# Gates and branch projections with tokens on partitions, in a two-layer hybrid encoder on one core

## The chip, the cores and the metric

The kernel runs on one core of a Trainium2 chip. The metric is the device time of one execution in microseconds (us). The engines named here are TensorE (PE, matmuls; PEld is its weight load), VectorE (DVE), ScalarE (ACT), GpSimd (POOL) and SyncE (SP, which here issues nearly all DMA transfers). Each engine works through its own list of instructions in order and waits on semaphores where it needs another engine's result.

## The reference

Two layers over 256 tokens of width 1024, in float32. Each layer has a token mixer and a gated MLP, each with an RMSNorm ahead and a residual sum behind. The mixer, which is the part that matters here:

```python
u, q, k, v, g_pool, g_attn = jnp.split(xn @ w_in, SPLITS, axis=-1)
pool_out = einsum(centred means of u at windows 2, 4, 8, 16, minus u; w_pool) * pool_scale
# three groups of four heads, (window, dilation) = (128,1), (512,4), (2048,16)
logits = q . k over +-64 strided keys / sqrt(128) + T5 bias;  p = softmax(logits)
attn = sum over the groups of softmax(lse over the groups) * (p @ v)      # 256 x 512
merged = sigmoid(g_pool) * (pool_out @ w_a) + sigmoid(g_attn) * (attn_out @ w_b)
h = h + merged @ w_o
```

The MLP is `(gelu(conv3(a)) * gval) @ w_down` with `a, gval` from `xn @ w_up`.

## The kernel before

**Arithmetic.** Every float32 operand of a large product is split in two parts, a rounded one (`h` in a name, for high) and the rest (`l`, low), and three products stand for one: high by high, high by low, low by high. The weights are split on the chip: a load of 1 MB lands in one of three `raw` buffers, ScalarE casts a piece of 128x1024 to `wh` (L177), VectorE subtracts to give `wl` (L178). Two pieces come from one load, and there are five `wh`/`wl` buffers; `W.get` hands out the next piece and splits up to three ahead, in the order in which `W.use` listed them.

**Layouts.** A product can leave its result in one of two layouts. In `proj` (L491 and L493, in `two_sums`) the weights are stationary and the tokens stream: the result has 128 channels on partitions and 256 tokens along the row, 8 matmuls with 512 columns and 8 with 256. In `v_sum` (L588) the normed tokens `x2` are stationary and the weights stream: the result has 128 tokens on partitions and 512 channels along the row. Tokens are split by parity: t = 0 holds the even ones, t = 1 the odd ones.

**Order of a layer.** Values (`v_sum`); the pool branch's `u`; then the queries and keys by `PAIRS`, two heads a visit; the four heads of attention; the projection of the pool branch by w_a into `pa`; the pool gate; the attention gate with the product by w_b; `residual_mm` with w_o; the norm; the MLP.

**Attention.** Four steps per head hh (each head stands for three, one of each group). `scores` (L886, L891) makes logits on TensorE, and VectorE and ScalarE make the softmax (L897, L902, L905, L908). `turn` transposes inside 32x32 blocks on VectorE (L915) into `rows` and then `cross` moves the blocks between groups of partitions by 16 transfers within SBUF, 32 KB each, all issued by SP (L598), into `pt`. `parts` casts and subtracts (L929, L930). `weigh` multiplies by the values (L939, L943) into `at2`. A list `steps` holds them as scores a, scores b, turn a, parts a, weigh a, turn b, parts b, weigh b for the pairs (0, 1) and (2, 3), and `step()` takes the next one after a projection. There is one `rows` and one `pt` buffer.

**Gates and merge.** `gate(c)` makes 128 channels of a gate by `proj`, adds the two sums (`add_up`: L513 on ScalarE, L514 on VectorE) and takes tanh (L1009); sigmoid is (tanh(x/2) + 1)/2, with the halves folded into the pool scale and the softmax scaling. The pool side is multiplied at L1014. For the attention side the product by w_b is made for 128 channels at a time (`b_ps`), multiplied (L1030), added to `pa` (L1033) and split into `mh`, `ml` (L1035, L1036). So the merged rows arrive with channels on partitions, as `residual_mm` (L518 to L520, `res_ps`) wants them: stationary operands of 128 channels by 128 tokens. `residual_mm` takes its eight channel blocks k in order: for k = 0 to 3 all four sums (two parities, two halves of the width); it holds k = 4 to 7 and finishes one sum after another, so that the norm can begin with the first (L423, then `xn` at L450 and the turn at L459).

**What orders the work.** The Python program says what follows what, and the framework's planner, which goes by its own costs, fixes each engine's list when the kernel is built; it may place instructions of one step between those of another. SP's list is in order too: a load that waits for its buffer holds back all transfers behind it. A transfer also waits for the transfer eight before it, which used the same semaphore.

Of the kernel before, what the change touches and what calls it, by code (L numbers as in the profile page):

```python
# [16 lines left out]
P = 128  # L17
D = 1024
# [20 lines left out]
LAG = 6  # L39
ENTRY = 4  # L40
# [164 lines left out]
def encoder(ctx, tc, x, w_in, w_pool, pool_scale, w_a, w_b, w_o, norm1, norm2, w_up, conv_w,  # L205
# [29 lines left out]
    for l in range(DEPTH):  # L235
# [10 lines left out]
        for n, c in enumerate(PAIRS):  # L246
            pool = ([], [])
            if n == 1:
                pool = W.add(
                    w_pool[l].rearrange("g (k p) c -> p (g k) c", p=P), (8, 256),  # L250
                    [((lambda t, j=j: t[:, 4 * j : 4 * j + 4, :]), (4, 256)) for j in range(2)],
                )
                pool = (pool[:1], pool[1:])
            W.use(pool[0] + cols(w_in[l], C_Q + c * 256))
            W.use(pool[1] + cols(w_in[l], C_K + c * 256))
        for c in range(4):
            W.use(cols(w_a[l], c * 256))
        for c in range(4):
            W.use(cols(w_in[l], C_GP + c * 256))
        for c in range(2):  # L260
            W.use(cols(w_in[l], C_GA + c * 512))
            W.use(cols(w_in[l], C_GA + c * 512 + 256))
            src = w_b[l][:, c * 512 : (c + 1) * 512].rearrange("(k p) c -> p k c", p=P)
            W.use(
                W.add(
                    src, (4, 512),
                    [((lambda t, j=j: t[:, :, j * 256 : (j + 1) * 256]), (4, 256)) for j in (0, 1)],
                )
            )
# [313 lines left out]
    def v_sum(ps, x2, t, n, piece):  # L583

        _, (wh, wl) = piece
        passes = [(0, wh, 0), (0, wl, 0), (1, wh, 0), (0, wh, 1), (0, wl, 1), (1, wh, 1)]
        for m, (part, w, j) in enumerate(passes):
            nc.tensor.matmul(  # L588
                ps, x2[:, 2 * n + j, part, t, :], w[:, j, :], start=(n + m == 0),
                stop=(n == 3 and m == 5),  # L590
            )

    def cross(out, in_):

        for i in range(4):
            for j in range(4):
                a, b = slice(32 * i, 32 * i + 32), slice(32 * j, 32 * j + 32)
                nc.sync.dma_start(out=out[b, i], in_=in_[a, j])  # L598

# [165 lines left out]
    for l in range(DEPTH):  # L765
# [113 lines left out]
        probs, ptiles = {}, {}  # L879
# [32 lines left out]
        def turn(hh):  # L912
# [6 lines left out]
            pt = sm.tile([P, 4, 2, 4, 32], F32, tag="pt", bufs=1, name="pt")  # L919
            cross(pt, rows)  # L920
            ptiles[hh] = pt
# [29 lines left out]
        steps = []  # L951
        for a, b in ((0, 1), (2, 3)):
            steps += [(scores, a), (scores, b), (turn, a), (parts, a), (weigh, a)]
            steps += [(turn, b), (parts, b), (weigh, b)]

        def step():
            if steps:
                f, *which = steps.pop(0)
                f(*which)


        for m, c in enumerate(PAIRS):
# [7 lines left out]
            for n in range(4):  # L970
                if m == 1:
                    next(pool_parts)
                src, rest = (halves(a) for a in proj(x2))
# [19 lines left out]
                if m >= 3 and n and len(steps) > 8:  # L993
                    step()

        pa = big.tile([P, KD, S], F32, tag="ybig", name="pa")
        for c in range(KD):
            add_up(pa[:, c, :], proj(po2))
            step()
        assert not steps  # L1000
# [3 lines left out]
        gates = big.tile([P, 4, S], F32, tag="gates", name="gates")  # L1004

        def gate(c):
            th = gates[:, c % 4, :]
            add_up(th, proj(x2))
            nc.scalar.activation(th, th, AF.Tanh, scale=0.5)  # L1009
            return th  # L1010

        for c in range(KD):
            th = gate(c)
            nc.vector.scalar_tensor_tensor(  # L1014
                out=pa[:, c, :], in0=th, scalar=1.0, in1=pa[:, c, :], op0=ALU.add, op1=ALU.mult
            )
        m2 = big.tile([P, 2, KD, 2, P], F32R, tag="m2", name="m2")
        mh, ml = m2[:, 0], m2[:, 1]
        for c4 in range(2):
            ths = [gate(4 * c4 + j) for j in range(4)]  # L1020
            for j2 in range(2):
                i, (wh, wl) = W.get()
                for j in range(2):
                    c = 4 * c4 + 2 * j2 + j
                    ps = mmp.tile([P, 2, S], F32, tag="mm", name="b_ps")
                    cc = slice(j * P, (j + 1) * P)
                    two_sums(ps, lambda k: wh[:, k, cc], lambda k: wl[:, k, cc], at2, 4)
                    m = sm.tile([P, S], F32, tag="u", name="m")
                    add_up(m, (ps[:, 0], ps[:, 1]))
                    nc.vector.scalar_tensor_tensor(  # L1030
                        out=m, in0=ths[2 * j2 + j], scalar=1.0, in1=m, op0=ALU.add, op1=ALU.mult
                    )
                    nc.vector.tensor_add(out=m, in0=m, in1=pa[:, c, :])  # L1033
                    m = halves(m)
                    nc.scalar.copy(out=mh[:, c], in_=m)  # L1035
                    nc.vector.tensor_sub(out=ml[:, c], in0=m, in1=mh[:, c].bitcast(F32))  # L1036
                W.free(i)
# [154 lines left out]
```

## Time and profile before

| | |
|---|---|
| median of 3 runs | 887.76 us (885.21 to 887.93) |
| the profiled execution | 886.05 us, span 884.3 us |
| TensorE busy | 868.0 us (98%) |
| VectorE, ScalarE busy | 682.5 us (77%), 518.7 us (59%) |
| DMA | 168.86 MB, mean 191 GB/s; queue q1's packets take 57% of 16 engines' span |

The page's groups have one line each: source line, engine, operation, output <- input, partitions x elements, count; then the busy time in us, the mean of one in ns, and the idle time of that engine just ahead of it with what ended it. A chain follows the work that ended last back to its causes: start, length, what. "SPq" is time in which SP issues transfers. By stretch, each engine has its busy time and, in brackets, its number of instructions; PEclk is the granted share of TensorE's clock. Matmuls overlap: one of 128x512 shows 0.39 us while the next starts 0.23 us behind it, so starts are to be compared, not lengths.

### The profile page before, as it was taken

What the parts mean: (1) busy time and instruction counts of PE and PEld (TensorE: products, weight loads), DVE (VectorE), ACT (ScalarE), POOL (GpSimd) and SP (SyncE); (2) the same over time, 40 slices, a digit from 0 to 9 for tenths busy, and PEclk for the clock granted to TensorE, in tenths of its full rate; (3) what the DMA queues carried; (4) which work ended last, traced back from release to release, by engine and by line L of the source; (5) the groups of instructions that cost most, each with busy time, mean ns of one, the idle gap of its engine ahead of it and who ended that gap; (6) DMA issues with size and microseconds to landing.
All of it is one profiled execution on the core that took longest, in us unless ns stands there. A gap on an engine that the chain in (4) does not pass through costs nothing.

```text
span 884.3 us, 12920 instructions
## 1 busy us (share of the span) xinstructions
PE 868.0 (98%) x4778; PEld 752.8 (85%) x4778; DVE 682.5 (77%) x1150; ACT 518.7 (59%) x905; POOL 14.7 (2%) x45
## 2 busy tenths in 40 slices
PE   9999999999999999999999999999999999999997
PEld 7888887888888888888888898888888888888886
DVE  6997785857869987787756977776678698878774
ACT  6755553556648766666545564554566486656653
POOL 2000000000000000000000000000000000000000
PEclk9999999999999999999999999999999999999999
DMA  9669636466564665565626465544755447556541
GB/s 326 214 232 297 226 117 196 157 222 208 179 207 146 208 219 191 165 215 191 238 96 237 144 215 168 170 164 135 269 188 191 158 155 247 182 191 199 182 143 49
DMA packets 132236, 168.86 MB, mean 191 GB/s; under 512 B 5302, under 2 KB 112518, under 8 KB 132044
## 3 DMA queue, kind: packets, MB, share of 16 engines
q1 hardware_dynamic: 132156, 168.02, 57.0%
q8 instruction: 38, 0.62, 0.3%
q14 instruction: 26, 0.21, 0.1%
q10 hardware_dynamic: 16, 0.00, 0.0%
HBM read 162.74 MB, written 3.69 MB: 188 GB/s over the span
## 4 chain that ended last, share of the span: by engine, by line
PE 82%; SPq 8%; DMA 3%; DVE 3%; issue 1%; ACT 1%; ACTq 0%; POOLq 0%; POOL 0%; DVEq 0%
PE proj_ps L491 30%; PE proj_ps L493 16%; SPq L598 8%; PE res_ps L518 6%; PE v_ps L588 6%; PE res_ps L519 6%; PE res_ps L520 6%; PE v_ps L757 2%; PE b_ps L491 2%; DMA pt<-rows 2%; PE v_ps L670 1%; DMA raw<-in_w_in_dram 1%; PE o_ps L939 1%; PE o_ps L943 1%; PE b_ps L493 1%
## 5 line engine op out<-in xcount | busy, mean ns | idle before, releaser
L178 DVE TENSOR_TENSOR wl<-raw,wh 128x1024 fp32r<-128x1024 f32 x274 | 333.8, 1223 | 121.5 <-ACT wh L177 119.6
L177 ACT CAST wh<-raw 128x1024 fp32r<-128x1024 f32 x274 | 286.1, 1049 | 183.0 <-PE proj_ps L491 113.6
L491 PE MATMUL proj_ps<-x,wh 128*128 128x512 f32 x1408 | 353.2, 392 | 0.0
L491 PEld LDWEIGHTS proj_ps<-x,wh 128*128 128x128 f32 x1408 | 254.1, 189 | 46.0
L493 PEld LDWEIGHTS proj_ps<-x,wl 128*128 128x128 f32 x1408 | 192.5, 190 | 13.8
L493 PE MATMUL proj_ps<-x,wl 128*128 128x256 f32 x1408 | 197.6, 282 | 0.0
L518 PE MATMUL res_ps<-wh,actq 128*128 128x512 f32 (+1 forms) x184 | 70.2, 381 | 0.0
L519 PE MATMUL res_ps<-wl,actq 128*128 128x512 f32 (+1 forms) x184 | 70.1, 381 | 0.0
L520 PE MATMUL res_ps<-wh,actk 128*128 128x512 f32 (+1 forms) x184 | 69.9, 380 | 0.0
L520 PEld LDWEIGHTS res_ps<-wh,actk 128*128 128x128 f32 x184 | 34.6, 188 | 6.7
L518 PEld LDWEIGHTS res_ps<-wh,actq 128*128 128x128 f32 x184 | 34.7, 188 | 6.2
L519 PEld LDWEIGHTS res_ps<-wl,actq 128*128 128x128 f32 x184 | 34.7, 188 | 6.0
L491 PE MATMUL proj_ps<-po,wh 128*128 128x512 f32 x128 | 33.6, 396 | 0.0
L1122 ACT ACTIVATE y<-y 128x256 f32<-128x256 f32 x44 | 18.3, 416 | 24.4 <-DVE y L1119 24.2
L1105 ACT ACTIVATE y<-a,prm 128x256 f32<-128x256 f32 x36 | 21.6, 599 | 16.1 <-DVE a L514 16.1
L425 ACT ACTIVATE junk<-h 128x512 f32<-128x512 f32 (+1 forms) x20 | 10.9, 547 | 27.7 <-DVE h L423 27.7
L518 PE MATMUL res_ps<-wh,m 128*128 128x512 f32 (+1 forms) x72 | 26.5, 368 | 0.0
L519 PE MATMUL res_ps<-wl,m 128*128 128x512 f32 (+1 forms) x72 | 26.3, 366 | 0.0
L520 PE MATMUL res_ps<-wh,m 128*128 128x512 f32 (+1 forms) x72 | 26.3, 365 | 0.0
L491 PEld LDWEIGHTS proj_ps<-po,wh 128*128 128x128 f32 x128 | 22.7, 189 | 3.7
L588 PE MATMUL v_ps<-wh,x 128*128 128x512 f32 x80 | 25.7, 392 | 0.0
L1106 DVE SCALAR_TENSOR_TENSOR y<-a,prm,y 128x255 f32<-128x255 f32 x36 | 17.3, 481 | 8.1 <-ACT y L1105 8.1
(205 smaller groups left out, 1094.6 us busy)
## 6 DMA issues: line engine op xcount, KB each, us to landing
raw<-in_w_in_dram SPq DMA_DIRECT2D x58, 1024.0 KB
raw<-in_w_up_dram SPq DMA_DIRECT2D x44, 1024.0 KB
raw<-in_w_down_dram SPq DMA_DIRECT2D x22, 1024.0 KB
raw<-in_w_a_dram SPq DMA_DIRECT2D x8, 1024.0 KB
raw<-in_w_o_dram SPq DMA_DIRECT2D x8, 1024.0 KB
pt<-rows SPq DMA_DIRECT2D x128, 32.0 KB
raw<-in_w_b_dram SPq DMA_DIRECT2D x4, 1024.0 KB
sk<-fd SPq DMA_DIRECT2D x1, 2560.0 KB
```

The source lines that it names most:

```text
L177: lambda: nc.scalar.copy(out=h, in_=src),
L178: lambda: nc.vector.tensor_sub(out=l, in0=src, in1=h.bitcast(F32)),
L491: nc.tensor.matmul(ps, wh(k), x2[:, k], start=(k == 0), stop=False)
L493: nc.tensor.matmul(ps[:, 1], wl(k), x2[:, k, 0], start=False, stop=(k == nk - 1))
L518: nc.tensor.matmul(ps, ah, wh, start=first, stop=False)
L519: nc.tensor.matmul(ps, ah, wl, start=False, stop=False)
L520: nc.tensor.matmul(ps, al, wh, start=False, stop=last)
L588: nc.tensor.matmul(ps, x2[:, 2 * n + j, part, t, :], w[:, j, :], start=(n + m == 0), stop=(n == 3 and m == 5),)
L598: nc.sync.dma_start(out=out[b, i], in_=in_[a, j])
L757: nc.tensor.matmul(ps[t], a[:, k, t, :], w[:, j, :], start=(k + m == 0), stop=(k == KD - 1 and m == 2),)
L1105: nc.scalar.activation(y, a, AF.Identity, bias=b, scale=w1)
L1122: nc.scalar.activation(y2, y2, AF.Tanh, scale=c)
```

## The change

Gates and the two branch projections are made with tokens on partitions. `by_rows` runs `v_sum` for both parities over the pieces of 512 channels, with the weights listed as row pieces of 512 columns. The pool gate comes first now, then w_a, then the attention gate and w_b per half of the width. tanh and the products work on 128 tokens by 512 channels, straight from PSUM. So the merged rows come out with tokens on partitions and must be turned for `residual_mm`: the first half of the width by one VectorE transpose in 32x32 blocks and a `cross` of 16 transfers (`merged_parts`, a step after each piece of the second half), the second half by 16 VectorE transposes of 32 partitions each (`blocks`).

Attention's steps get fixed visits (`VISITS`: for scores, turn, parts and weigh the visit of each head). There are 28 visits, one after each projection from the fourth pair on and one after each row piece of the pool gate and w_a. `cross` became a generator that yields after four transfers, and each visit asks for four more. `pt` is one tile for two heads, in other tiles' places. In the second pair of heads the pool step follows the projection instead of preceding it, and the pool weights stand between the two pieces of a load in the list.

```diff
+VISITS = ((0, 3, 12, 13), (1, 5, 13, 17), (6, 10, 18, 22), (7, 11, 19, 23))
...
+        for w, c0 in ((w_in[l], C_GP), (w_a[l], 0)):
+            for half in HALVES:
+                for j in range(2):
+                    W.use(rows(w, j * 512, 4, c0 + half.start, 512))
+        for half in HALVES:
+            for j in range(2):
+                W.use(rows(w_in[l], j * 512, 4, C_GA + half.start, 512))
+            W.use(rows(w_b[l], 0, 4, half.start, 512))
...
+    def by_rows(x2, of, visit=None):
+        ps = [mmp.tile([P, 512], F32, tag="mm", name="rows_ps") for _ in range(2)]
+        for n in range(of):
+            piece = W.get()
+            for t in range(2):
+                v_sum(ps[t], x2, t, n, piece, of)
+            W.free(piece[0])
+            if visit:
+                visit()
+        return ps
...
     def cross(out, in_):
         for i in range(4):
             for j in range(4):
                 a, b = slice(32 * i, 32 * i + 32), slice(32 * j, 32 * j + 32)
                 nc.sync.dma_start(out=out[b, i], in_=in_[a, j])
+            yield
+
+    def blocks(out, in_):
+        for i in range(4):
+            for j in range(4):
+                a, b = slice(32 * i, 32 * i + 32), slice(32 * j, 32 * j + 32)
+                nc.vector.transpose(out=out[b, :, :, a], in_=in_[a, :, :, b])
...
+            if hh % 2 == 0:
+                ptiles["pair"] = big.tile(
+                    [P, 2, 4, 2, 4, 32], F32, tag=("ybig", "xn")[hh // 2], name="pt"
+                )
+            ptiles[hh] = ptiles["pair"][:, hh % 2]
+            crossing.append(cross(ptiles[hh], rows))
...
         def step():
-            if steps:
-                f, *which = steps.pop(0)
-                f(*which)
+            for f, hh in visits.pop(0):
+                f(hh)
+            if crossing and next(crossing[0], "end") == "end":
+                crossing.pop(0)
...
-                if m >= 3 and n and len(steps) > 8:
+                if m >= 3:
                     step()
...
+        for n, cc in enumerate(HALVES):
+            ps = by_rows(x2, 4, step)
+            if n == 0:
+                pa = big.tile([P, 2, D], F32, tag="q1", name="pa")
+            for t in range(2):
+                nc.scalar.activation(pa[:, t, cc], ps[t], AF.Tanh, scale=0.5)
+        for cc in HALVES:
+            ps = by_rows(po2, 4, step)
+            for t in range(2):
+                p = pa[:, t, cc]
+                nc.vector.scalar_tensor_tensor(
+                    out=p, in0=p, scalar=1.0, in1=ps[t], op0=ALU.add, op1=ALU.mult
+                )
...
+        way = big.tile([P, 2, 4, 2, 4, 32], F32, tag="k1", name="way")
+        def merged_parts():
+            yield from cross(way[:, 1], way[:, 0])
+            yield
+            for t in range(2):
+                m = way[:, 1, :, t].rearrange("p i c r -> p c i r")
+                hi, lo = (a[:, 0:4, t].rearrange("p c (i r) -> p c i r", i=4) for a in (mh, ml))
+                nc.scalar.copy(out=hi, in_=m)
+                nc.vector.tensor_sub(out=lo, in0=m, in1=hi.bitcast(F32))
+
+        for n, cc in enumerate(HALVES):
+            ps = by_rows(x2, 4, n and (lambda: next(first, None)))
+            th = big.tile([P, 2, 512], F32, tag=("q0", "k0")[n], name="th")
+            for t in range(2):
+                nc.scalar.activation(th[:, t], ps[t], AF.Tanh, scale=0.5)
+            ps = by_rows(at2, 2, n and (lambda: next(first, None)))
+            for t in range(2):
+                p = th[:, t]
+                nc.vector.scalar_tensor_tensor(
+                    out=p, in0=p, scalar=1.0, in1=ps[t], op0=ALU.add, op1=ALU.mult
+                )
+                nc.vector.tensor_add(out=p, in0=p, in1=pa[:, t, cc])
+            if n == 0:
+                nc.vector.transpose(
+                    out=way[:, 0].rearrange("p j t c r -> p (t c) j r"),
+                    in_=th.rearrange("p t (c j r) -> p (t c) j r", c=4, j=4),
+                )
+                first = merged_parts()
+            else:
+                assert next(first, None) is None
+                turned = big.tile([P, 4, 2, P], F32, tag="v0", name="turned")
+                blocks(
+                    turned.rearrange("p c t q -> p t c q"), th.rearrange("p t (c k) -> p t c k", c=4)
+                )
+                for k in range(0, 4, 2):
+                    hi, lo = (a[:, 4 + k : 6 + k] for a in (mh, ml))
+                    nc.scalar.copy(out=hi, in_=turned[:, k : k + 2])
+                    nc.vector.tensor_sub(out=lo, in0=turned[:, k : k + 2], in1=hi.bitcast(F32))
```

74 lines of the change are left out of this document (12 added, 62 removed).

## The prediction

> **What bounds the kernel now.** First the page's busy list, then busy time by stretch, then what TensorE waits for.
>
> ```profile
> PE 868.0 (98%) x4778; PEld 752.8 (85%) x4778; DVE 682.5 (77%) x1150; ACT 518.7 (59%) x905; POOL 14.7 (2%) x45
> ```
> ```profile
> core 0: us, PE busy (x) PEld busy (x) DVE busy (x) ACT busy (x) POOL busy (x), PEclk, DMA share, GB/s
> 108.49:191.20 82.71, 78.92 (x482) 69.52 (x481) 58.62 (x97) 39.44 (x75) 0.00 (x0) 1.00 0.47 153
> 191.20:235.81 44.61, 44.61 (x258) 39.18 (x256) 34.68 (x60) 29.38 (x59) 0.00 (x0) 1.00 0.66 226
> 544.00:625.80 81.80, 77.18 (x474) 67.96 (x473) 56.98 (x95) 39.11 (x73) 0.00 (x0) 1.00 0.48 155
> 625.80:670.00 44.20, 44.20 (x254) 38.76 (x253) 34.37 (x60) 28.99 (x57) 0.00 (x0) 1.00 0.66 226
> ```
> ```profile
> PE o_ps L939 <- ACT pth L929: 8.3, 7, 1.9
> ```
>
> TensorE is the bound. Its idle time sits in one place per layer: the attention stretch, 82.71 - 78.92 = 3.8 us in layer 0 and 81.80 - 77.18 = 4.6 in layer 1. The seven waits of `weigh` for `parts` are 8.3 us of that. A wait loses a little more than it shows, since idle time begins 0.16 us after the next matmul was due (a 128x512 matmul shows 0.39 us and follows the last one by 0.23), so I count 8.4 + 7 x 0.16 = 9.5 us lost. In the gate stretches (191.20 and 625.80) TensorE never stops. The chain shows what `parts` waits for:
>
> ```profile
> 111.29 0.36 PE s_ps L886 x3
> 112.89 1.85 PE proj_ps L491 x8
> ...
> 123.42 0.59 SPq L598
> 124.06 0.59 SPq L598
> ...
> 131.67 1.39 SPq L598
> 133.10 1.89 DMA pt<-rows
> 135.01 0.41 ACT pth L929
> 135.47 0.38 PE o_ps L939
> ```
>
> One `cross` is 16 issues at 0.633 us (124.06 - 123.42), 10.1 us of SP's queue, then 1.9 to land and 0.4 for the first cast: 12.4 us from transpose to `weigh`. One `scores` is 1.6 us of TensorE.
>
> **Part 1: the projections by rows.**
>
> ```profile
> 450.54 27.23 PE v_ps L588 x120
> 480.54 1.84 PE proj_ps L491 x8
> 483.33 1.84 PE proj_ps L491 x8
> ```
> ```profile
> 213.41 1.09 PE L491 MATMUL b_ps<-at,wh 128*128 128x512 f32 x4
> 219.02 2.00 PE L491 MATMUL proj_ps<-x,wh 128*128 128x512 f32 x8
> ```
>
> A `proj` is 2.79 us (483.33 - 480.54). A piece by rows is 12 matmuls of the form of `v_sum`, at 27.23 / 120 = 0.227: 2.72. Per layer 16 gate pieces and 8 of w_a save 0.07 each, 1.7; the four w_b pieces cost 5.61 / 2 = 2.80 and save 0.08 each, 0.3. Two layers: **-4.0 us**, all on the path. The form already runs in this kernel with the same weights and tokens, so the bounds are narrow (-3.5 to -4.5).
>
> The sums, tanh and products that shrink on ScalarE and VectorE are worth nothing: the gate stretches have no idle TensorE, whose 44.61 us cover VectorE's 34.68; without that cover they would be some of VectorE's 10 us to spare there. Loads in row pieces, the pool weights' new place, and `pa`, `th` and `pt` in other tiles also cost nothing while the five wh/wl buffers stay ahead of TensorE; if a piece came late, 2.4 us (a cast, a subtraction) would show.
>
> **Part 2: attention at fixed visits.** The prices are:
>
> ```profile
> L177 ACT CAST wh<-raw 128x1024 fp32r<-128x1024 f32 x274 | 286.1, 1049 | 183.0 <-PE proj_ps L491 113.6 <-PE res_ps L520 32.8 <-DMA raw<-in_w_in_dram 11.5
> L905 ACT ACTIVATE probs<-probs,nm 128x512 f32<-128x512 f32 x16 | 11.4, 718 | 5.8 <-DVE nm L902 5.7
> L462 ACT CAST x<-xt_ps 128x512 fp32r<-128x512 f32 x12 | 7.0, 584 | 11.8 <-PE xt_ps L459 11.8
> ```
> ```profile
> L178 DVE TENSOR_TENSOR wl<-raw,wh 128x1024 fp32r<-128x1024 f32 x274 | 333.8, 1223 | 121.5 <-ACT wh L177 119.6
> L897 DVE TENSOR_TENSOR probs<-s_ps,bt 128x512 f32<-128x512 f32 x16 | 10.6, 684 | 0.1
> L902 DVE TENSOR_REDUCE nm<-probs 128x1 f32<-128x512 f32 x16 | 10.5, 679 | 0.1
> L915 DVE STREAM_TRANSPOSE rows<-probs 128x1024 f32<-128x1024 f32 x8 | 9.9, 1239 | 9.0 <-DMA pt<-rows 9.0
> L908 DVE TENSOR_SCALAR probs<-probs,rz 128x512 f32<-128x512 f32 x16 | 7.6, 477 | 0.1
> L930 DVE TENSOR_TENSOR ptl<-pt,pth 128x256 fp32r<-128x256 f32 x16 | 5.9, 411 | 4.4 <-ACT pth L929 4.3
> L423 DVE TENSOR_TENSOR h<-res_ps,h 128x512 f32<-128x512 f32 x12 | 8.3, 688 | 8.3 <-PE res_ps L520 8.3
> L385 DVE COPY fsb<-f_ps 4x256 f32<-4x256 f32 x5 | 1.9, 409 | 0.1
> ```
>
> With `pt` in pairs a `cross` need no longer wait until the previous `weigh` has read `pt`. But the built program's instruction order still shows head 0's and head 2's 16 issues in one run, and it puts the next head's transpose ahead of this head's `ptl` on VectorE. TensorE runs no other product between the six `weigh` products of head 0 and only a few inside the other heads'. I follow each head, in us after `scores` has left TensorE:
>
> Head 0: until its transpose ends VectorE does the adds, maxima and scalings, two weight splits and five query/key sums, 8.5; then 10.1 + 1.9 + 0.4 gives 20.9. TensorE arrives after seven projections and a `scores`, 7 x 2.79 + 1.6 = 21.1. But `ptl` comes after head 1's transpose (1.2), and its second half after a key sum whose cast stands behind a weight cast (1.05 + 0.38): 22.2 and 23.6. Lost: 2.0.
>
> Head 1: its transfers land in time, but on ScalarE `pth` is queued behind a weight cast whose buffer TensorE gives back only 1.4 us before `weigh`; cast, key copy, `pth` (1.05 + 0.38 + 0.4), then `ptl` behind that weight's subtraction. Lost: 1.1.
>
> Head 2: heads 2 and 3 score close together, so the transpose ends at 8.3, the transfers land at 20.4, and TensorE arrives at 1.6 + 7 x 2.72 = 20.6. `pth` is ready at 20.9, `ptl` stands behind head 3's transpose and a split: 23.2. Lost: 2.2.
>
> Head 3: SP issues 12 of 16, then a w_in load that waits for its raw buffer; the last four follow it, and `pth` stands behind the cast of that load. Lost: 1.9.
>
> On SP the weight loads behind a `cross` start up to 10.1 us later; the three raw buffers and five wh/wl buffers keep them early except at heads 1 and 3, as counted. POOL's queue isn't touched. Together 7.2 a layer, 14.4 in all against 9.5 now: **+4.9 us**. Each of the eight can be off by 1 us and they lean the same way: I bound the total lost by 7 and 22 (-2.5 to +12.5).
>
> **Part 3: turning the merged rows.** Now no step is late there: `res_ps` begins at 235.81, straight behind `b_ps`. In the change, take 0 as the end of the last product with w_b. Half one: its two sums finish 2.25 us after its own w_b products (four passes at 0.6), one split and the transpose follow (1.15 + 1.2), so `way` is ready at 4.6. SP then issues 12 transfers, a weight load and 4 more, 17 x 0.633 = 10.8, and they land 1.9 later: 17.4 us. TensorE has only 72 x 0.227 = 16.3 us of work left: they land at about +1.1.
>
> ```profile
> GB/s 199 250 332 379 385 383 381 389 381 389 389 361 174 66 55 23 53 66 66 59 23 66 66 64 35 33 66 66 59 18 229 211 342 354 385 389 377 385 387 387
> ...
> raw<-in_w_a_dram SPq DMA_DIRECT2D x1, 1024.0 KB
> ```
>
> The load in the middle moves 1 MB at 385 GB/s, 2.7 us, and lands at about the same time. ScalarE takes its cast first (1.05), then `merged_parts`' cast (0.6): the first `res_ps` starts at +2.7 instead of 0. Its low half comes in time, as TensorE has four products that need none.
>
> Half two: `blocks` are 16 transposes of 32x256. No row has that form. By size they cost as a quarter of 1.24, 0.31; the longest reading is 1.24 each. A copy of 4x256 takes 0.41, so the length of the row sets the price, not the partitions; of two 128x256 steps in a row (0.75) the second adds 0.33:
>
> ```profile
> 236.21 0.75 DVE L1030 SCALAR_TENSOR_TENSOR m<-gates,m 128x256 f32<-128x256 f32 x2
> ...
> 250.17 0.68 DVE L423 TENSOR_TENSOR h<-res_ps,h 128x512 f32<-128x512 f32 x1
> ```
>
> I take 0.34 each, as the nearest row, 5.5 us together, from +4.0 (sums and `merged_parts`' subtractions) to +9.5. Two splits (2.3) and ScalarE's casts stand between, so the parts come at 11.8 to 13. TensorE wants them at 2.7 + 4 x 2.72 + 0.45 = 14.1: hidden. VectorE's backlog then makes the first `h` sum, 14.4 us behind the first `res_ps` now (250.17), about 1 us later, against some 0.7 of slack before `xt_ps`: 0.3. So 3.0 a layer, **+6.0 us**. Bounds: 1.5 a layer if SP has no pause, 5.5 if two pauses like the 1.39 us issue above fall in a `cross` and the splits queue worse.
>
> The Trainium skill, "VectorE: DVE Perf Modes", section "Two Vector instructions with no wait between them", says in a model of its own that an instruction whose output starts in another group of 32 partitions than the last one starts only when everything before it has finished. By that rule the 16 transposes, each to another group, cost the full 0.42, 1.3 us more, of which 0.7 a layer would reach TensorE, and the sum would be 1.4 us higher; no run here shows it.
>
> **The sum.** -4.0 + 4.9 + 6.0 = +6.9 on the profiled execution's 886.05 us (span 884.3): 893.0. That execution is 1.7 us under the median of 887.76; half of that added, I say **894**. Ends: -4.5 - 2.5 + 3 gives 882, -3.5 + 12.5 + 11 gives 906.
>
> **Rivals.** (1) Faster: the paired `pt` frees the transfers early enough for every `parts` to be ready. Then the 9.5 us go and none come back: 886.05 - 9.5 - 4.0 + 6.0 = 878.5. For it: SP's wait for `weigh` goes, and the landings I get are within 1 us of TensorE's arrival. Against: `ptl` stands behind another transpose on VectorE, whatever lands. It decides once attention loses under 7 us in all. (2) No change: attention loses what it does now and the tail 2 a layer: 886.
>
> (3) A stop slows TensorE's clock. The rows above give 1.00 in every stretch, and after a wait of 1.9 us too:
>
> ```profile
> 130.00:136.00 6.00, 4.11 (x26) 3.54 (x25) 2.69 (x4) 2.33 (x5) 0.00 (x0) 1.00 0.29 73
> ```
>
> If the gap ahead of `res_ps`, at 2.7 us the longest, were followed by 3.4 us at half clock, 1.7 us a layer would be lost more: 897.5. The Trainium skill, "TensorE: Matmul & The Clock Gate", section "Why this matters for your kernels", wants no gaps over about 3 us; the trace, with none so long, can't show it. (4) The 16 transposes cost 1.24 each: 14.3 us more, 2 of them hidden, 24 us in all: 918.
>
> **Chances.** Forecast 0.58, faster 0.22, no change 0.10, clock 0.06, dear transposes 0.04. The measurement tells apart about 0.3%, 2.7 us. So faster 0.22, same 0.10, slower 0.68. The forecast's own range is 889 to 903; with the other cases, 0.1 left out at either end, 879 to 904.
>
> **What would show it.** Right: by-rows matmuls 0.227 us apart; `weigh` waiting for `pth` or `ptl` 12 to 15 us in all; TensorE idle 2 to 4 us at the first `res_ps` of each layer, behind the cast of `merged_parts`; no stop at k = 4. Wrong: no wait at `res_ps` (the transfers landed sooner than 17.4 us), a wait in its middle (the transposes are dear), or `weigh` waiting under 7 us.

## The result, and the profile after

The changed kernel takes 887.74 us (median of 20 executions, 885.86 to 891.05), the kernel before, on the same chip, 885.57 (20 executions, 884.38 to 888.08). The ratio is 1.0023, with a 95% interval of 1.0014 to 1.0032: 2 us slower, a quarter of a per cent. The forecast was 894, with a range of 889 to 903: the sign was right, and the change forecast, +6.9 us, was three times too large.

The profiled execution of the changed kernel shows less than that: 886.12 us with a span of 884.3, where the one before had 886.05 and the same 884.3. So there are two questions. Why do the parts add up to nothing, where +6.9 was forecast? And where do the 1.6 us between this execution and the median come from?

First the page's busy list and three stretches of layer 0, the attention stretch, the gates up to the last product with w_b, and the start of the residual products.

```profile
PE 864.0 (98%) x4554; PEld 739.7 (84%) x4554; DVE 674.0 (76%) x1088; ACT 498.2 (56%) x817; POOL 15.6 (2%) x45
```
```profile
core 0: us, PE busy (x) PEld busy (x) DVE busy (x) ACT busy (x) POOL busy (x), PEclk, DMA share, GB/s
108.40:192.10 83.70, 81.37 (x452) 70.16 (x451) 58.92 (x90) 40.73 (x68) 0.00 (x0) 1.00 0.53 177
192.10:232.10 40.00, 40.00 (x177) 32.85 (x175) 22.36 (x23) 17.30 (x19) 0.00 (x0) 1.00 0.57 181
232.10:250.00 17.90, 14.72 (x62) 11.33 (x62) 17.02 (x29) 8.28 (x10) 0.00 (x0) 1.00 0.53 185
```

TensorE has 4 us less to do (864.0 against 868.0), and attention now leaves it idle for 83.70 - 81.37 = 2.3 us in place of 3.8. What was won is lost in the third stretch, 17.90 - 14.72 = 3.2 us. TensorE's waits (total, times, longest):

```profile
PE res_ps L514 <- ACT m L1042: 5.6, 2, 2.9
PE o_ps L958 <- DVE ptl L949: 3.7, 4, 1.7
PE pool_ps L479 <- DVE po L881: 1.3, 1, 1.3
PE o_ps L958 <- ACT pth L948: 1.1, 2, 0.7
...
PE res_ps L515 <- DVE wl L179: 1.0, 4, 0.3
```

The wait of `weigh` fell from 8.3 to 4.8 us. New are the wait of the first `res_ps` of each layer, 5.6, and 1.0 in four pieces among the residual products. At the pool products of layer 0 the wait is 1.3, where the kernel before had 0.2. Two rows of the chain of work (start, duration): the matmuls by rows take 21.14 / 93 = 0.227 us, as forecast, and half one's last transfer lands at 234.18.

```profile
192.06 21.14 PE rows_ps L584 x93
...
230.28 3.90 DMA way<-way
```

The third stretch, in the timeline of PE, of ACT and of DVE (start, duration; in brackets the idle time ahead and what ended it):

```profile
231.84 0.39 PE L584 MATMUL rows_ps<-wh,at 128*128 128x512 f32 x1
234.93 0.50 PE L514 MATMUL res_ps<-wh,m 128*128 128x512 f32 x1 [2.70 <-ACT m L1042]
```
```profile
233.14 1.04 ACT L178 CAST wh<-raw 128x1024 fp32r<-128x1024 f32 x1 [2.54 <-DVE th L1053]
234.25 1.14 ACT L1042 CAST m<-way 128x512 fp32r<-128x512 f32 x2
```
```profile
234.91 1.29 DVE L1043 TENSOR_TENSOR m<-way,m 128x512 fp32r<-128x512 f32 x2 [0.65 <-ACT m L1042]
236.12 7.17 DVE L614 STREAM_TRANSPOSE turned<-th 32x256 f32<-32x256 f32 x16
```

TensorE is through at 232.07 (231.84 and 0.23 for the last matmul), and half one's parts exist from 234.9 on. The 16 transposes of half two take 7.17 us, 0.448 each. The products that need them begin at 246.0 and wait for nothing, though with little to spare. But the weight splits that stand behind the transposes on VectorE are late: the four waits of 0.2 to 0.3 us at L515 are theirs.

Sum: -4.0 for the rows, -3.7 for attention (9.5 lost before; 4.8 of idle time and six beginnings of 0.16 now, 5.8), +5.9 for the two stops (5.6 and 2 x 0.16), +1.1 for the pool products and +1.0 for the four small waits. That is +0.3, against 0.07 measured between the two profiled executions.

### The profile page after: what moved, and what is told of

Its sections match the earlier page's. It is cut to its first block, busy times and chain, and to the rows that moved or that the text cites. A ratio compares the mean times of both kernels' runs of the same rounds, so it can differ in the third digit from the quotient of the medians.

```text
span 884.3 us, 12329 instructions
## 1 busy us (share of the span) xinstructions
PE 864.0 (98%) x4554; PEld 739.7 (84%) x4554; DVE 674.0 (76%) x1088; ACT 498.2 (56%) x817; POOL 15.6 (2%) x45
## 4 chain that ended last, share of the span: by engine, by line
PE 79%; DVE 7%; DMA 6%; SPq 5%; issue 1%; ACT 1%; POOLq 0%; DVEq 0%; ACTq 0%; POOL 0%
PE proj_ps L487 25%; PE proj_ps L489 13%; PE rows_ps L584 10%; PE v_ps L584 6%; PE res_ps L515 5%; PE res_ps L516 5%; PE res_ps L514 5%; SPq L606 5%; DMA raw<-in_w_in_dram 4%; PE v_ps L773 2%; DVE wl L179 2%; DVE turned L614 2%; PE v_ps L686 1%; ACT wh L178 1%; PE o_ps L962 1%
## 5 line engine op out<-in xcount | busy, mean ns | idle before, releaser
L487 PE MATMUL proj_ps<-x,wh 128*128 128x512 f32 x1152 | 288.8, 392 | 0.0
L487 PEld LDWEIGHTS proj_ps<-x,wh 128*128 128x128 f32 x1152 | 208.2, 189 | 38.0
L489 PEld LDWEIGHTS proj_ps<-x,wl 128*128 128x128 f32 x1152 | 157.2, 190 | 11.3
L489 PE MATMUL proj_ps<-x,wl 128*128 128x256 f32 x1152 | 160.8, 282 | 0.0
L584 PE MATMUL rows_ps<-wh,x 128*128 128x512 f32 x256 | 81.7, 392 | 0.0
L515 PE MATMUL res_ps<-wl,actq 128*128 128x512 f32 (+1 forms) x184 | 70.1, 381 | 0.0
L584 PEld LDWEIGHTS rows_ps<-wh,x 128*128 128x128 f32 x256 | 48.1, 188 | 9.7
L584 PE MATMUL rows_ps<-wl,x 128*128 128x512 f32 x128 | 49.8, 389 | 0.0
L584 PE MATMUL rows_ps<-wh,po 128*128 128x512 f32 x128 | 40.3, 391 | 0.0
L515 PEld LDWEIGHTS res_ps<-wl,actq 128*128 128x128 f32 x184 | 34.7, 188 | 6.0
L514 PE MATMUL res_ps<-wh,m 128*128 128x512 f32 (+1 forms) x72 | 26.8, 372 | 5.6 <-ACT m L1042 5.6
L584 PEld LDWEIGHTS rows_ps<-wl,x 128*128 128x128 f32 x128 | 24.1, 188 | 4.7
L515 PE MATMUL res_ps<-wl,m 128*128 128x512 f32 (+1 forms) x72 | 26.8, 373 | 1.0 <-DVE wl L179 1.0
```

The lines of the kernel that those rows point to most:

```text
L487: nc.tensor.matmul(ps, wh(k), x2[:, k], start=(k == 0), stop=False)
L489: nc.tensor.matmul(ps[:, 1], wl(k), x2[:, k, 0], start=False, stop=(k == nk - 1))
L514: nc.tensor.matmul(ps, ah, wh, start=first, stop=False)
L515: nc.tensor.matmul(ps, ah, wl, start=False, stop=False)
L584: nc.tensor.matmul(ps, x2[:, 2 * n + j, part, t, :], w[:, j, :], start=(n + m == 0), stop=(n == of - 1 and m == 5),)
```

## The experiments

Each starts from the changed kernel, and each median stands beside runs of the kernel before on the same chip, whose median was 886.0 to 886.4.

**The kernel before, run as it is.**

> The kernel before itself, to see the granted clock of its executions, one by one, beside the times. Theory C (the new stop ahead of res_ps costs TensorE's clock in some executions): all of these executions carry 0.996 to 0.999, and the time lies within 1 us of 885.6. Rival (the clock's spread belongs to the chip or the hour, not to the change): clocks of 0.990 to 0.995 show up here too, with times 2 to 4 us longer, as in the changed kernel.

Its 11 executions have clocks of 0.997 to 0.999, and the 29 that other kernels were compared with 0.996 to 0.999, median 0.998. The 20 of the changed kernel go from 0.990 to 0.999, median 0.9945, and their time follows: the four at 0.999 took 885.9 to 886.7, the two slowest (0.990 and 0.991) 891.1 and 890.3. The spread came with the change, which speaks for C. The run with the pool products back (below) has the same long stops and goes from 0.991 to 0.999 beside the same 29, so it isn't the chip.

**Half one's transfers from two queues.**

```diff
-    def cross(out, in_):
+    def cross(out, in_, queues=(nc.sync, nc.sync)):
...
-                nc.sync.dma_start(out=out[b, i], in_=in_[a, j])
+                queues[j % 2].dma_start(out=out[b, i], in_=in_[a, j])
...
-            yield from cross(way[:, 1], way[:, 0])
+            yield from cross(way[:, 1], way[:, 0], (nc.sync, nc.gpsimd))
```

> Only the merged rows' 16 transfers are issued from two queues, SP and POOL by turns, instead of SP alone; attention's transfers are left. Theory A (the issues, one after the other on SP, are what is late at the first res_ps): the transfers land 4 to 5 us sooner and the two waits there, 5.6 us, go: median 887.7 - 5.6 = 882. Rival B (the transfers are bound by the 1 MB weight loads beside them): they land under 1 us sooner, the waits stay over 4 us, and the time falls by less than 1.5 us. If theory C holds as well, another 1.5 to 2 us goes with the clock: 880.

885.71 us, ratio 0.9991 [0.9978, 1.0003]: not to be told from the kernel before, where 882 was expected. The chain of work has this:

```profile
224.81 0.52 SPq L606
225.37 4.93 DMA way<-way
```

The last transfer lands at 230.30, 3.9 us sooner than from one queue, so A is right in that, and the first `res_ps` no longer waits. But the stop has moved on:

```profile
PE res_ps L514 <- ACT m L1071: 3.6, 2, 2.1
PE res_ps L516 <- DVE m L1072: 1.0, 2, 0.5
```

These are the casts and subtractions of half two, at k = 4. The 16 transposes end no sooner (244.6 against 243.3), while TensorE arrives 2.7 us earlier. In the changed kernel the late transfers of half one cover the late transposes of half two: two things are late here, one just behind the other.

**The stop filled with matmuls** (into a PSUM tile that nobody reads).

```diff
+        junk = mmp.tile([P, 512], F32, tag="mm", name="junk_ps")
+        for k in range(10):
+            nc.tensor.matmul(junk, at2[...], at2[...], start=(k == 0), stop=(k == 9))
         run(residual_mm(...))
```

> Ten matmuls of 128x512 into a PSUM tile that nobody reads stand between the last product with w_b and the first res_ps, 10 x 0.227 = 2.3 us, so that TensorE is busy for most of the stop of 2.7 to 2.9 us; everything else is as in the changed kernel. Theory C (the stop costs clock in some executions): the stop shrinks to about 0.5 us, the clocks return to 0.997 or more, and the median falls by 1.5 to 2 us, to 886. Rival (the stop costs only itself): the median stays within 0.7 us of 887.7.

The stop shrank to 0.9 us and the clocks went back to 0.996 to 0.999, as C says; but there are five executions only. The time rose to 889.56, ratio 1.0036 [1.0023, 1.0048], so neither expected median came true. The last transfer landed 0.5 us later than without the filling (4.40 us behind the start of its issue, 3.90 there), and a new wait of 1.9 us in all stands ahead of `xt_ps`. So the clock answers to the stop; the price of the clock can't be read from this kernel.

**The pool products back ahead of the projection.**

```diff
-                W.use([a] + pool[j] + [b])
+                W.use(pool[j] + [a, b])
...
+                if m == 1:
+                    next(pool_parts)
                 src, rest = (halves(a) for a in proj(x2))
-                if m == 1:
-                    next(pool_parts)
```

> The pool products go back ahead of the projection, and their weights ahead of both of the query's or key's pieces, as in the kernel before; the rest is as in the changed kernel. Theory D (the 1.3 us wait of pool_ps in layer 0 came with that move): the wait goes and the time falls by 1.3 us, to 886.4. Rival: VectorE's two splits stand ahead of the pool parts in either order, the wait stays or moves to the next product, and the time stays within 0.5 us.

888.2 us, ratio 1.0019 [1.0006, 1.0031]: no gain. The 1.3 us wait went, as D said, but 0.9 + 0.5 us of waits for `pll` and `plh` came in its place. (The kernel before waits for `pll` too, 0.2 us in its first profiled execution and 0.9 in the one of its run above.) But the profiled execution, at a mean clock of 0.993 and with a span of 888.3, shows what the clock does. Its windows, and then those of the changed kernel's profiled execution around the same stop:

```profile
core 0: us, PE busy (x) PEld busy (x) DVE busy (x) ACT busy (x) POOL busy (x), PEclk, DMA share, GB/s
234.00:237.00 3.00, 0.37 (x2) 0.30 (x2) 2.42 (x5) 1.93 (x3) 0.00 (x0) 1.00 0.96 352
237.00:241.00 4.00, 4.00 (x12) 3.10 (x11) 3.92 (x9) 0.16 (x1) 0.00 (x0) 0.57 0.79 310
...
674.00:678.00 4.00, 4.00 (x13) 3.11 (x12) 3.89 (x10) 0.92 (x1) 0.00 (x0) 0.57 0.46 180
173.00:175.00 2.00, 0.35 (x3) 0.30 (x3) 1.98 (x4) 0.59 (x2) 0.00 (x0) 1.00 1.05 407
176.00:180.00 4.00, 4.00 (x15) 3.33 (x14) 1.56 (x2) 1.11 (x2) 0.00 (x0) 0.57 0.65 216
```
```profile
232.00:235.00 3.00, 0.30 (x3) 0.07 (x1) 2.35 (x5) 1.79 (x3) 0.00 (x0) 1.00 1.03 356
235.00:239.00 4.00, 4.00 (x18) 3.27 (x19) 3.92 (x9) 1.38 (x2) 0.00 (x0) 1.00 0.84 327
```

Behind the stop of layer 0 (234 to 237), that of layer 1 (the row of 674) and that of head 2 (173 to 175) come 4 us in which only 12 to 15 matmuls begin in place of 18, at a mean clock of 0.57: 0.43 x 4 / 0.5 = 3.4 us at half clock. The same stop of the changed kernel has none behind it. Three such stretches lose 3 x 1.7 = 5.1 us; 4.0 of them show against the span of 884.3. One stretch lowers the mean clock by 1.7 / 884 = 0.0019, so the changed kernel's median clock, 0.0045 under 0.999, stands for 2.3 of them. In time they show less than 1.7 us each: a straight line through the changed kernel's 20 executions gives 0.7 us for 0.0019 of clock, and the median lies 1.6 us above the profiled execution, not 2.3 x 1.7 = 3.9. Where the rest is saved isn't shown.

**Attention as before**, the rest of the change kept.

```diff
-            if hh % 2 == 0:
-                ptiles["pair"] = big.tile([P, 2, 4, 2, 4, 32], ...)
-            ptiles[hh] = ptiles["pair"][:, hh % 2]
-            crossing.append(cross(ptiles[hh], rows))
+            ptiles[hh] = sm.tile([P, 4, 2, 4, 32], F32, tag="pt", bufs=1, name="pt")
+            run(cross(ptiles[hh], rows))
...
+            steps += [(scores, a), (scores, b), (turn, a), (parts, a), (weigh, a)]
+            steps += [(turn, b), (parts, b), (weigh, b)]
```

> Attention alone goes back to the kernel before: its list of steps, one at a time, 16 transfers in one go, one pt buffer; by_rows, the pool step's place and the merged rows stay as in the changed kernel. Theory E (the fixed visits and the paired pt gained what the traces show: 9.5 us lost before, 5.9 now): +3.6 us, median 891, and the waits of weigh are again above 8 us. Rival (the prediction's working: the new attention loses 14.4 against 9.5): -4.9 us, 882.8.

896.12 us, ratio 1.0122 [1.0095, 1.0150]. The clocks are 0.985 to 0.999. The profiled execution is the fastest, 892.46 at a clock of 0.999; its span of 890.4 is 6.1 over the changed kernel's, and these are waits of TensorE in it:

```profile
PE o_ps L954 <- ACT pth L944: 9.2, 7, 2.0
PE res_ps L514 <- ACT m L1036: 5.6, 2, 3.0
...
PE o_ps L954 <- DVE ptl L945: 1.2, 2, 0.6
```

`weigh` waits 10.4 us where the changed kernel's waits 4.8. E holds, and more than it said: the attention part of the change is worth 6 us at full clock. (The old steps lose more here than the 8.3 us of the kernel before, so this is more than the 3.7 of the sum.) It is the term that the forecast had at +4.9.

**One `pt` buffer, the visits kept.**

```diff
-            if hh % 2 == 0:
-                ptiles["pair"] = big.tile([P, 2, 4, 2, 4, 32], ...)
-            ptiles[hh] = ptiles["pair"][:, hh % 2]
+            ptiles[hh] = sm.tile([P, 4, 2, 4, 32], F32, tag="pt", bufs=1, name="pt")
```

> The fixed visits stay, but pt is one buffer again, for all heads. Theory F (the pair is what counts): the transfers of heads 1 and 3 can't start until weigh of heads 0 and 2 has read pt, two visits or 5.6 us later; with 1.5 us to spare, each loses some 4 us, 16 in all: about 903, with SP's queue held up. Rival (the order of the visits is what counts): within 1.5 us of the changed kernel.

890.86 us in the one execution, at a clock of 0.997:

```profile
PE o_ps L954 <- ACT pth L944: 4.5, 4, 1.3
PE o_ps L954 <- DVE ptl L945: 4.4, 4, 1.6
```

8.9 us against 4.8 with the pair and 10.4 with the old steps: the pair is worth 4.1 of the 5.6 us of waits; the visits, with their transfers by fours, 1.5. F is right on what counts and four times too dear.

**Head 3 two visits later.**

```diff
-VISITS = ((0, 3, 12, 13), (1, 5, 13, 17), (6, 10, 18, 22), (7, 11, 19, 23))
+VISITS = ((0, 3, 12, 13), (1, 5, 13, 19), (6, 10, 18, 24), (7, 11, 19, 25))
```

> Head 3's turn, parts and weigh come two visits later (19, 24, 25 instead of 17, 22, 23), so that its transpose no longer stands ahead of head 2's ptl on VectorE. Theory G (that transpose of 1.25 us is what makes head 2's wait of 1.65): the wait shrinks to under 0.6 in both layers, 2 us less, and one stop less that can cost clock: median 885 to 886. Rival (head 2's wait is bound by the transfers' landing): it stays within 0.3 us of 1.65, and the time within 0.7 us of 887.7.

887.47 us, ratio 1.0016 [1.0007, 1.0026], and head 2's wait stays at 1.6. This tells nothing of G: the planner set head 3's transpose ahead of head 2's `ptl` all the same (171.93 and 174.21 on VectorE). A visit number doesn't fix an engine's order.

**Transposes to the partitions that they read.** The blocks land in wrong rows, so this kernel serves for timing only.

```diff
-                nc.vector.transpose(out=out[b, :, :, a], in_=in_[a, :, :, b])
+                nc.vector.transpose(out=out[a, :, :, b], in_=in_[a, :, :, b])
```

> Each of the 16 transposes of half two writes to the 32 partitions that it reads, so that 12 of 16 write to the same group of 32 partitions as the one before (the blocks land in the wrong rows; the amount of work is the same). Theory H (an instruction on VectorE whose output goes to another group of partitions starts only when the one before has finished): the pitch falls from 0.448 us to about 0.34 for the 12. Rival (the pitch is the price of the form): 0.448 for all 16. The span doesn't change by more than 0.5 us, either way, since they are hidden.

The row on VectorE:

```profile
238.04 5.69 DVE L614 STREAM_TRANSPOSE turned<-th 32x256 f32<-32x256 f32 x16
```

5.69 us in place of 7.17. If the four that change group still take 0.448, the other twelve take (5.69 - 1.79) / 12 = 0.33. H holds. The rule that the prediction drew from the Trainium skill ("VectorE: DVE Perf Modes", section "Two Vector instructions with no wait between them"), that an instruction whose output starts in another group of 32 partitions waits for all before it, agrees with this case: 0.448 against 0.33. What it costs TensorE (0.7 a layer, by the prediction) isn't seen: this is one execution, at a clock of 0.992.

**Half one earlier.** Half two's product with w_a and its gate go behind half one's product with w_b.

```diff
-        for w, c0 in ((w_in[l], C_GP), (w_a[l], 0)):
-            for half in HALVES:
...
+        for half in HALVES:
+            half_of(w_in[l], C_GP, half)
+        for half in HALVES:
+            half_of(w_a[l], 0, half)
+            half_of(w_in[l], C_GA, half)
             W.use(rows(w_b[l], 0, 4, half.start, 512))
```

(and the products in the same order)

> Half two's product with w_a and its gate of attention now stand behind half one's product with w_b, so that 10 pieces, 27 us of TensorE, cover half one's transfers instead of 16.3; both halves are turned as in the changed kernel. Theory T (half one's transfers are late because too little work covers them): the first res_ps of each layer waits no more, -5.6 us. But half two's 16 transposes (7.2 us, behind 2.3 us of sums, with 2.4 of weight splits between) are then the next late thing: TensorE wants their parts 11.3 us after the last product with w_b and they come at 12 to 13, so 0.5 to 2 us per layer come back at k = 4: 884 to 886. Rival: the wait stays at over 4 us, since the landing is bound by the loads beside it; 887 to 888.

882.48 us, ratio 0.9950 [0.9933, 0.9967]. T holds. No wait of the first `res_ps` is left, and at k = 4 the waits are small:

```profile
PE res_ps L518 <- DVE m L1074: 0.9, 2, 0.5
PE res_ps L517 <- DVE wl L179: 0.6, 2, 0.3
PE res_ps L516 <- ACT m L1073: 0.4, 2, 0.2
```

1.9 us for both layers, within the 1 to 4 expected; the median lies 1.5 under the range. The four clocks are 0.997 to 0.999.

**And half two turned by TensorE.**

```diff
-                blocks(
-                    turned.rearrange("p c t q -> p t c q"), th.rearrange("p t (c k) -> p t c k", c=4)
-                )
+                    for j in range(2):
+                        for t in range(2):
+                            c0 = (k + j) * P
+                            nc.tensor.transpose(ps[:, j, t, :], th[:, t, c0 : c0 + P], ident)
```

(two groups per layer, ahead of the products of k = 2 and k = 3)

> As the one before, and half two is turned by TensorE: 8 matmuls of 128x128 with the identity per layer between the products of k = 1 and k = 3, instead of 16 transposes on VectorE. Theory T: no wait at the first res_ps nor at k = 4; TensorE pays 8 x 0.11 = 0.9 us a layer, so -5.6 + 1.8 = -3.8, and two long stops fewer to cost clock (mean clock 0.995 or more in most executions): median 882 to 884. Rival (VectorE's backlog or the new order makes another stop): over 886.

881.36 us, ratio 0.9940 [0.9922, 0.9958], 0.6 better than expected, with no wait left at `res_ps` and clocks of 0.996 to 0.999. Against the order alone it gains 1.1 us in the medians of four executions each, which is within their spread.

**Head 3's transpose held until head 2's `ptl` is issued.**

```diff
+                if hh == 3:
+                    queued.enter_context(tc.issue_after(last_ptl[0].ins))
                 nc.vector.transpose(
```

(with visits 19, 23 and 24 for head 3)

> The changed kernel with head 3's transpose held on VectorE until head 2's ptl has been issued (its visits are 19, 23 and 24); the rest is as it was. Theory G (that transpose, 1.25 us, stands in the way of head 2's ptl): head 2's wait falls from 1.65 to under 0.6 us in each layer, 2 us less: 885.7, with the clock's dip behind that stop gone as well. Rival: the wait moves to head 3 or stays; within 0.7 us of 887.7.

884.53 us, ratio 0.9980 [0.9966, 0.9995], 1.2 better than expected. Two visits later alone had left the order as it was, so it is the hold that counts. VectorE of the changed kernel around head 2, and then of this one:

```profile
171.69 1.25 DVE L931 STREAM_TRANSPOSE rows<-probs 128x1024 f32<-128x1024 f32 x1 [2.35 <-DMA pt<-rows]
172.86 1.18 DVE L179 TENSOR_TENSOR wl<-raw,wh 128x1024 fp32r<-128x1024 f32 x1
173.97 0.75 DVE L949 TENSOR_TENSOR ptl<-pt,pth 128x256 fp32r<-128x256 f32 x2
```
```profile
172.40 0.76 DVE L952 TENSOR_TENSOR ptl<-pt,pth 128x256 fp32r<-128x256 f32 x2
173.08 1.24 DVE L934 STREAM_TRANSPOSE rows<-probs 128x1024 f32<-128x1024 f32 x1
```

All waits of `weigh` together are 1.2 us in place of 4.8. G holds. The stops ahead of `res_ps` are still there (6.2, the longest 3.2), and every one of the seven clocks is 0.994 to 0.996, no higher than the changed kernel's median: the expected gain in clock isn't seen.

**Both together**: the new order, half two turned by TensorE, and head 3's transpose held.

> The two before together: the new order, half two turned by TensorE, and head 3's transpose behind head 2's ptl. If both theories hold and add up: -3.8 - 2 and fewer dips of the clock: median 880 to 882, faster than both kernels, and clocks of 0.997 or more. Rival: one of the two gains is taken back at head 3 or at the pool step; 883 or more.

875.74 us, ratio 0.9877 [0.9862, 0.9891]: 1.2% faster than the kernel before, and 4 us under the expected range. The page's busy list and all waits but those of the first microseconds:

```profile
PE 863.6 (99%) x4570; PEld 741.5 (85%) x4570; DVE 661.2 (76%) x1056; ACT 498.6 (57%) x817; POOL 15.5 (2%) x45
```
```profile
PE pool_ps L481 <- DVE po L883: 1.1, 1, 1.1
...
PE o_ps L963 <- ACT pth L953: 0.5, 1, 0.5
PE o_ps L963 <- DVE ptl L954: 0.5, 2, 0.3
```

2.1 us of waits in place of 12.7, which accounts for the 10.5 us between the profiled executions (875.65 and 886.12). The four clocks are 0.998 to 0.999. The waits add up: the new order with TensorE's turns takes away 6.7 us of them, the held transpose 3.9, both together 10.6. The medians gain a little more than that: against the changed kernel's 2.2 us above the kernel before, the parts stand 7.1 and 3.9 us lower, and both together 12.7. The parts run at clocks of 0.994 to 0.999 and the whole at 0.998 to 0.999, so the clock is the likely reason for the other 1.7; no run shows it by itself.

| kernel | stops of TensorE of 1.5 us and more | executions | clock: lowest, median, highest | median us |
|---|---|---|---|---|
| before | 1 of 1.9 to 2.05 | 67 | 0.996, 0.998, 0.999 | 886.0 to 886.4 |
| changed | 2 of 2.7 to 2.9, 2 of 1.5 to 1.65 | 20 | 0.990, 0.9945, 0.999 | 887.74 |
| two queues | 2 of 1.5 to 2.1, 2 of 1.5 to 1.65 | 11 | 0.993, 0.997, 0.999 | 885.71 |
| stop filled | 2 of 1.5 to 1.65 | 5 | 0.996, 0.998, 0.999 | 889.56 |
| pool products back | 2 of 2.6 to 2.9, 2 of 1.5 to 1.65 | 12 | 0.991, 0.995, 0.999 | 888.2 |
| attention as before | 2 of 2.6 to 3.0, 4 up to 2.0 | 6 | 0.985, 0.9935, 0.999 | 896.12 |
| head 3 two visits later | 2 of 2.8 to 3.1, 2 of 1.5 to 1.65 | 11 | 0.991, 0.994, 0.997 | 887.47 |
| head 3 held | 2 of 3.0 to 3.2 | 7 | 0.994, 0.995, 0.996 | 884.53 |
| new order | 2 of 1.5 to 1.65 | 4 | 0.997, 0.998, 0.999 | 882.48 |
| new order, TensorE turns | 2 of 1.5 to 1.65 | 4 | 0.996, 0.9965, 0.999 | 881.36 |
| both | none | 4 | 0.998, 0.999, 0.999 | 875.74 |

Clocks under 0.996 occur only in kernels with a stop longer than that of the kernel before (2.05 us). In the profiled executions of the changed kernel and of the runs after it, 8 of the 14 stops of 2.5 to 3.2 us ahead of `res_ps` are followed by a stretch at half clock, 4 of the 9 stops of 1.65 us at head 2 of layer 0, and none of the 9 of 1.5 us at head 2 of layer 1. So a single execution can show several stretches or none.

## Why the prediction was right or wrong

**Part 1, -4.0: right.** 0.227 us a matmul, TensorE's busy time 4.0 us lower. That the pool weights' new place costs nothing didn't come out: 1.3 us at the pool products of layer 0, where two weight splits (82.57 to 84.9 on VectorE) stand ahead of `po`. To undo the place alone gave 1.4 us of other waits, so the place alone isn't the reason; which of VectorE's steps there could go wasn't tried.

**Part 2, +4.9: wrong, and the step that made the forecast too large.** 14.4 us lost were forecast, 5.8 measured, which is outside this term's own bounds of 7 to 22: the term is 8.6 us off, more than the whole forecast was. By heads, in layer 0:

```profile
131.39 0.28 PE L958 MATMUL o_ps<-pth,vh 128*128 128x256 f32 x1
...
146.18 0.39 PE L958 MATMUL o_ps<-pth,vh 128*128 128x256 f32 x1 [0.41 <-ACT pth L948]
147.53 0.39 PE L958 MATMUL o_ps<-ptl,vh 128*128 128x256 f32 x1 [0.28 <-DVE ptl L949]
...
174.44 0.38 PE L958 MATMUL o_ps<-ptl,vh 128*128 128x256 f32 x1 [1.65 <-DVE ptl L949]
...
190.04 0.28 PE L958 MATMUL o_ps<-pth,vh 128*128 128x256 f32 x1
```

Heads 1 and 2 came out in size: 1.1 and 2.2 forecast, 1.0 and 1.8 measured. At head 2 it is the very transpose named, as the held transpose shows. At head 1 `pth` does stand behind a weight cast and a key copy, but that cast (144.50 on ScalarE) waited for its load to land, by the trace, and not for a buffer from TensorE: there the size is partly luck. Heads 0 and 3 were forecast at 2.0 and 1.9 and lose nothing.

Head 0: the transpose was to end 8.5 us behind `scores` and ended 7.1 behind (110.14 to 117.26), since one split and four sums were ahead of it, not two and five. The transfers landed 1.3 us behind the last issue, not 1.9:

```profile
117.42 10.09 SPq L606 DMA_DIRECT2D pt<-rows  x16
```
```profile
128.86 0.71 ACT L948 CAST pth<-pt 128x256 fp32r<-128x256 f32 x2 [2.47 <-DMA pt<-rows]
```

The halves of `ptl` then began at 19.9 and 21.0 us, where 22.2 and 23.6 were forecast for them, and TensorE arrived at 21.25 (131.39), as forecast (21.1). The products that need them come a little later still, so both were in time, the second by about 0.3 us.

Head 3: the order came as worked, twelve transfers, a w_in load, four more, and `pth` behind that load's cast:

```profile
187.48 1.05 ACT L178 CAST wh<-raw 128x1024 fp32r<-128x1024 f32 x1 [2.07 <-DMA raw<-in_w_in_dram]
188.43 0.70 ACT L948 CAST pth<-pt 128x256 fp32r<-128x256 f32 x2
```

But the load, which was to wait for its raw buffer, was issued at 181.72, right behind the twelfth transfer. `pth` was ready 0.9 us before TensorE arrived at 190.04, `ptl` 0.3 before its product. The prediction gives no working for its 1.9, so no more can be said of what was wrong in it.

The step that failed is thus the lateness of `parts` at heads 0 and 3: two positions in VectorE's queue and 0.6 us of landing at the one, a wait of SP that didn't come at the other.

So the first rival's mechanism was right, at a chance of 0.22: the pair frees the transfers, as the run with one `pt` shows. Attention lost under 7 us, the point at which this rival was to decide, but not nothing, as its price had it: the 5.8 us are most of what lies between its 878.5 and the profiled 886.12.

**Part 3, +6.0: right in size, 5.9, and partly by luck.** The two stops are 2.7 and 2.9, as forecast at 2.7. But the cast of the weight load (1.05), which I put between landing and `merged_parts`, ran before the landing (233.14), and the transfers landed 1 us later than I had (at +2.1 us, not +1.1): two misses of the same size that cancel. The 16 transposes cost 0.448, not 0.34, and their own products waited for nothing, as forecast. The first `h` sum slipped by 2 us and not by 1, without any stop at `xt_ps`, where I had 0.3. The four waits for a weight split, 1.0 in all, were not foreseen.

**The clock (the third rival, chance 0.06): wrong about what it is worth.** I read 1.00 behind a stop of 1.9 us and took it that such stops don't touch the clock. Stops of 1.65 us and more do in some executions. TensorE loses 1.7 us in a stretch, as priced; but the two or so of the median execution add only 1.6 us to its time. At a clock of 0.999 the change takes 885.9 to 886.7 in four executions, and the kernel before, in its 28 beside the experiments, 884.9 to 886.8: what the clock leaves of the difference is a few tenths.

So most of the 2 us by which the change is slower fits the clock, which the sum of the forecast left out; the terms of the sum come to +0.3. That the sign came out right is mostly luck.

What the Trainium skill says of it ("TensorE: Matmul & The Clock Gate", section "Part 1: The HAM clock gate (the "warmup" mystery)"), that activity is judged in free-running windows of 3.4 us and the array runs at half rate until one of them was busy, agrees with 3.4 us at half clock behind a stop, and with its being there in one execution and not in another. That it takes a gap of about 3 us, as the prediction quoted from the same page, doesn't agree: half clock follows head 2's stop of 1.65 us too.

## What to carry to other kernels

Where TensorE is the bound, count its stops by length and not only by their sum: here a stop of 1.65 to 3.2 us could be followed by half clock, and 1.7 us of TensorE's work, which a single profiled execution may not show; compare the clocks of all executions. When a late transfer is made earlier, look first at what is late just behind it: here two queues removed 5.6 us of stops and 4.6 came back just behind, while more cover for the first half and another engine for the second removed all of them. A margin that is worked out from four or five queue positions is no better than 2 us a head: the forecast allowed 1 us, and two heads of four were off by 1.9 and 2.0. Let the bounds of such a term reach down to nothing lost, and check which position the built order really gives.

## What was not expected of the hardware

- Stretches of 3.4 us at half clock follow stops of TensorE of 1.65 to 3.1 us in some executions and not in others of the same kernel. In the profiled execution with head 3 held, half clock lasts 6.8 us: it sets in at about 233, within a stop of 3.2 us that ends at 234.07.
- A 32x256 transpose on VectorE that writes to another group of 32 partitions than the last one takes 0.448 us, to the same group 0.33.
- Transfers of 32 KB from SBUF to SBUF land 1.3 us behind the end of their last issue in a quiet moment (127.5 to 128.9), and 3.3 us behind it beside weight loads of 1 MB (230.9 to 234.2). Two queues that issue them by turns halve the time of the issues (220.5 to 225.9, where one queue takes 220.3 to 230.9), but the last one then lands 4.9 us behind its start, in place of 3.9.
